# Seven products for six of nine row tiles in layer 0's down-projection of a two-layer encoder step

## The chip, the cores and the metric

The kernel runs on one core of a Trainium2 chip. The metric is device time in microseconds (us) of one execution, the median of several runs. TensorE (PE in the profile) does the matmuls, VectorE (DVE) and ScalarE (ACT) and GpSimd (POOL) the elementwise work, and all transfers between the chip's memory and its on-chip buffer are issued by SyncE (SP).

## The reference

One inference step of a two-layer encoder over 1024 prompt rows and 8 x 16 sample rows, 1152 rows of 1024 columns in all. Layer 0 uses windowed attention, layer 1 a chunk-band attention over a K/V that is projected once after layer 0. Each layer closes with a GEGLU ConvFFN:

```python
u = h @ w_up                     # 1024 -> 2 * 2816
y = conv_b + sum(conv_w[tap] * ue[:, tap:tap + T] for tap in range(3))
a, g = split(y, 2)
f = (gelu(g) * a) @ w_down       # 2816 -> 1024: the down-projection
x = layer_norm(alpha * x + (1 + gate) * f)
```

The change concerns `@ w_down` of layer 0. Everything is float32; the kernel gets float32 accuracy from reduced operands by splitting each into a high part (a cast) and a low part (the difference), and adding three products: low x high, high x low, high x high.

## The kernel before

The 1152 rows are nine tiles of 128; tile 8 holds the sample rows. The inner dimension 2816 is 22 chunks of 128 (`NFF`), or 11 pairs 2m, 2m+1 (`NK`). The stages follow one another: attention, output projection, `ffn` with its up stage and its down stage, for layer 0 and then layer 1. A planner that simulates the engines (`schedule_with_timeline_sim`) sets each engine's order from the program order and the dependences; `issue_after` pins single instructions. Each engine then runs its list in order, and a `Ring` hands out buffers in turn: a load into a slot waits until the last reader of that slot is done.

**Up stage.** Chunks 0 and 1 go through `plain`, chunks 2 to 21 through `spair`: the up-projection of a chunk and its gate in seven products instead of eight (a Strassen-Winograd scheme), whose weight sums `presum` forms on POOL. `conv_row` applies the convolution, `gated` gelu and the gate (one POOL multiply per chunk, L1357) and stores the chunk to `actD`. In layer 0 the up stage also streams adaLN weights (`ada`, L240) as background work through the same ring of raw slots. In layer 1, `act_sums` (L1370 to L1375) forms on POOL the sums of two chunks' activations and stores them to `actS`, and `weight_sums` (L1378 to L1386) the sums of two chunks of `w_down`, stored to `wT`; `wsum` lists the chunks at which they are placed.

**Down stage of layer 1** (`down2`). Rows 0 to 511 against rows 512 to 1023, and chunk 2m against 2m+1 and column half against column half, form a 2 x 2 block product in seven products (numbered 1 to 7) of 11 steps; tile 8 rides along as a plain fifth tile. A step's operands are read from `actD` or `actS` and from `w_down` or `wT`, split by ScalarE (L183) and VectorE (L194), and multiplied on line L1627.

**Down stage of layer 0** (`down`). Three groups of three tiles, `GR`, each over all 22 chunks with both column halves in six banks. `fetch` loads a whole weight chunk (512 kB; high part on ScalarE, low part on POOL) and three tiles of the chunk's activations (192 kB; low part on VectorE, L1495), and `mm` (L1502) does 18 matmuls of 512 columns. The last group keeps its last four chunks (`KEEP`) back and ends tile by tile, so that `tail` of one tile runs beside the next one's matmuls. `tail` adds the residual (L1521) and calls `norm_tail`: layer norm on VectorE, transposes on TensorE (L1043) and the hidden rows for the next stage, which go to `H` and to `hD`.

The next stage (`kv`) reads the tiles in the order in which the groups finish, forms its own sums of the hidden rows (`tsums`), and needs these for its K products (L1237).

Slots of the seven-product form are half a weight chunk (512 columns, high and low), made by `subslots`:

```python
def subslots(self, ws):
    return Ring([tuple(w[i][:, h * 512 : h * 512 + 512] for i in range(2)) for w in ws for h in range(2)])
```

Of the kernel before, what the change touches and what calls it, by code (L numbers as in the profile page):

```python
# [31 lines left out]
LV = ((0, 1, 2, 8, 3, 4, 5, 6, 7), (0, 1, 2, 6, 7, 8, 3, 4, 5))  # L32
GR = ((0, 1, 2), (6, 7, 8), (3, 4, 5))
GB = ((6, 7, 0, 1, 2, 3), (4, 5, 6, 7, 0, 1), (2, 3, 4, 5, 6, 7))
TBG = ((2, 3), (0, 1), (0, 1))
NPL = 2
NK = NFF // 2
TAILS = ({1: 8}, {0: 0, 2: 1, 5: 2, 8: 3}, {})
# [67 lines left out]
class Trunk:  # L106
# [255 lines left out]
    def vproj(self, l, qs, banks, tmp, cut=NT):  # L362
        ws = [[self.wload(self.I[("wv0", "wv1")[l]][q, i]) for i in range(2)] for q in qs]
        for part in (LV[l][:cut], LV[l][cut:]):
# [478 lines left out]
    def kv(self, hmring):  # L843
# [46 lines left out]
        order = (0, 1, 2, 6, 7, 8, 3, 4, 5)  # L890
# [361 lines left out]
    def ffn(self, l, xsrc, xdst, affs):  # L1252
# [18 lines left out]
        ys = Ring([F[:, o : o + 1152] for o in (10492, 6396, 7548)])  # L1271
        yact, ygate = ys.items[0], ys.items[1:3]
# [82 lines left out]
        def gated(j, ya, yg):  # L1355
            nc.scalar.activation(yg, yg, AF.Gelu_apprx_tanh)
            nc.gpsimd.tensor_mul(yg, yg, ya)  # L1357
            if l == 0 or j % 2:
                nc.sync.dma_start(self.actD[j], yg)
                if l:  # L1360
                    self.pend.append(j // 2)
            else:
                for r in (slice(0, 512), slice(1024, 1152)):
                    nc.sync.dma_start(self.actD[j][:, r], yg[:, r])

        def act_sums():
            for m in self.pend:
                a11, a21 = ygate[0][:, 0:512], ygate[0][:, 512:1024]
                a12, a22 = ygate[1][:, 0:512], ygate[1][:, 512:1024]
# [4 lines left out]
                for i in range(2):  # L1374
                    nc.sync.dma_start(self.actS[m, i], ygate[i][:, 0:1024])  # L1375
# [12 lines left out]
        def plain(j):  # L1388
            y = [yact, ygate[j % 2]] if l else [ys.next(), ys.next()]
# [8 lines left out]
        sub = self.subslots(self.wslots[3:4] + self.wslots[l:3])  # L1398
# [6 lines left out]
        def spair(j, loaded=None, src=None, ready={}):  # L1405
# [5 lines left out]
            def after(i, q):  # L1411
# [6 lines left out]
                if l and i == 1:  # L1418
                    act_sums()
                if l and i == 2 and j in wsum:  # L1420
                    with self.tc.issue_after(pairdma):
                        weight_sums(wsum.index(j))
                if q == 4:
                    y.append(ygate[j % 2] if l else ys.next())
# [3 lines left out]
            ya = yact if l else ys.next()  # L1428
            row(ua, j, 0, ya)
            gated(j, ya, y[0])  # L1430

        self.pend = []
        wsum = list(range(4, 9)) + list(range(10, NFF - 1, 2))
        for j in range(NPL):
            plain(j)
        if l:
            self.take_w0(F32)
# [25 lines left out]
        else:  # L1463
            self.down(l, xsrc, xdst, affs)

    def down(self, l, xsrc, xdst, affs):
        nc, I, F = self.nc, self.I, self.F
        z = Ring([F[:, o : o + 1024] for o in (1152, 2176, 3200)])
        self.hf = F[:, 4224:5248]
        self.zt = F[:, 5248:6272]  # L1470
        self.gateS, self.gateP = F[:, 6272:7296], F[:, 7296:8320]
        xr = Ring([F[:, o : o + 1024] for o in ((8320, 9344) if l else (8320,))])
        spare = F[:, 9344:10368]
        self.lng, self.lnb = F[:, 10368:11392], F[:, 11392:12416]
        narrow = self.ws
        slots = narrow.items + [F[:, 0:1024]]
        self.ws = Ring(slots + [self.hf if l else spare], slots + [F[:, 11644:12668], F[:, 8700:9724]])
        acts = Ring([(self.X1[:, i * 768 : i * 768 + 384], self.X1[:, i * 768 + 384 : i * 768 + 768]) for i in range(6)])
        ws = self.wslots
        order = [ws[2], ws[3], ws[0], ws[1]] + [tuple(self.X1[:, o + 1024 * a : o + 1024 * a + 1024] for a in range(2)) for o in (4608, 6656)]  # L1480
        if l == 0:
# [598 lines left out]
```

## Time and profile before

| | |
|---|---|
| median of 3 runs | 2729.5 us (2723.69 to 2732.46) |
| the profiled execution | 2725.63 us |
| its span, first to last instruction | 2723.8 us, 47309 instructions |
| TensorE busy, granted clock | 96%, 0.99 |
| VectorE, ScalarE, POOL busy | 71%, 50%, 39% |
| layer 0's up-stage products (L1237), from | 523.4 us of the span, up to the down stage |
| layer 0's down stage (first to last of L1502) | 1024.1 to 1304.6 us |
| layer 1's up-stage products (L1237), last | 2479.0 us |
| layer 1's down stage (first to last of L1627) | 2460.8 to 2707.9 us |

A row of the engine windows gives a stretch of the span, its length, each engine's busy time with its number of instructions, then the granted TensorE clock, the busy share of the DMA engines and what they moved. A row of the groups gives line, engine, operation, what is written and read, shape, count, then busy time, mean nanoseconds of one, idle time before it and what ended that. A row of the timeline gives start, length, engine, line, operation; in brackets the idle time before it and what ended it. A row of waits reads "engine, tile, line <- who it waited for: total, times, longest".

### The profile page before, as it was taken

The page shows a single profiled execution, that of the slowest core. Times are in us where ns is not written, and L with a number is a line of the kernel's source. Part 1 is how long each engine was busy: PE and PEld are TensorE (multiplying, and loading weights), DVE is VectorE, ACT ScalarE, POOL GpSimd, SP SyncE. Part 2 cuts the span into 40 slices and gives each one's busy share as a digit, 9 for nine tenths or more (in the row PEclk, how much of TensorE's full clock was granted, in tenths as well). Part 3 has the DMA queues.
Part 4 walks back from the last instruction along what each step waited for, and adds up shares of the span by engine and source line. Part 5 has one row for each costly group of instructions (what it writes and reads, how often), then busy time and mean ns, then how long its engine had stood idle before and what let it go on. Part 6 is the DMA issues. An engine that isn't in the chain of part 4 may idle for free. (4 is left out here: it accounts for less than half of the span.)

```text
span 2723.8 us, 47309 instructions
## 1 busy us (share of the span) xinstructions
PE 2626.5 (96%) x17394; PEld 2344.4 (86%) x17394; DVE 1936.0 (71%) x3846; ACT 1348.5 (50%) x2777; POOL 1068.0 (39%) x771
## 2 busy tenths in 40 slices
PE   7999889999999999999999999989989999999997
PEld 6997768989999998887898888867889999998886
DVE  4476767776677675757864677776878877878668
ACT  3475733443333344444446666672445554546553
POOL 3032523444434357675220121252467666552101
PEclk9999899999999999999999999989999999999999
DMA  9656434644444447666658556774445334349673
GB/s 330 205 156 204 143 111 169 229 164 141 143 155 139 153 138 242 221 219 217 248 189 275 147 150 192 204 241 139 162 148 186 139 126 140 122 145 307 215 238 124
DMA packets 229385, 498.29 MB, mean 183 GB/s; under 512 B 37441, under 2 KB 98961, under 8 KB 229153
## 3 DMA queue, kind: packets, MB, share of 16 engines
q1 hardware_dynamic: 229152, 495.27, 55.3%
q8 instruction: 137, 2.24, 0.3%
q14 instruction: 96, 0.78, 0.1%
HBM read 378.15 MB, written 126.47 MB: 185 GB/s over the span
## 5 line engine op out<-in xcount | busy, mean ns | idle before, releaser
L1237 PE MATMUL PS<-H,wh 128*128 128x256 f32 (+1 forms) x2304 | 352.0, 294 | 0.0
L1237 PEld LDWEIGHTS PS<-H,wh 128*128 128x128 f32 x2304 | 319.3, 188 | 0.0
L1197 DVE TENSOR_TENSOR F<-PS,F 128x256 f32<-128x256 f32 (+1 forms) x446 | 197.3, 452 | 156.0 <-PE PS L1237 149.3
L194 DVE TENSOR_TENSOR wl<-F,wh 128x512 fp32r<-128x512 f32 (+2 forms) x205 | 201.4, 994 | 44.8 <-ACT wh L183 44.4
L183 ACT CAST wh<-F 128x512 fp32r<-128x512 f32 (+3 forms) x221 | 135.5, 625 | 196.8 <-PE PS L1237 89.8
L1237 PE MATMUL PS<-H,wl 128*128 128x320 f32 (+1 forms) x1152 | 201.2, 295 | 6.5 <-DVE wl L194 4.0
L1237 PEld LDWEIGHTS PS<-H,wl 128*128 128x128 f32 x1152 | 168.7, 188 | 12.5 <-issue 5.9
L1237 PE MATMUL PS<-xa,wh 128*128 128x320 f32 (+1 forms) x1168 | 179.2, 294 | 0.0
L1237 PEld LDWEIGHTS PS<-xa,wh 128*128 128x128 f32 x1168 | 162.5, 189 | 0.0
L647 POOL TENSOR_TENSOR F<-F,x2r 64x512 f32<-64x512 f32 x62 | 79.2, 1278 | 206.9 <-DVE F L623 179.4
L1495 DVE TENSOR_TENSOR xa<-xa 128x384 fp32r<-128x384 f32 x66 | 97.7, 1492 | 81.9 <-ACT xa L183 80.3
L183 ACT CAST wh<-ws 128x512 fp32r<-128x512 f32 (+1 forms) x123 | 90.8, 744 | 110.9 <-PE PS L1237 49.3
L1357 POOL TENSOR_TENSOR F<-F 128x1152 f32<-128x1152 f32 x44 | 124.7, 2833 | 43.9 <-DVE F L1350 21.3
L313 PE MATMUL PS<-H,w0r 128*128 128x384 f32 (+1 forms) x720 | 136.9, 340 | 0.0
L1286 DVE SCALAR_TENSOR_TENSOR F<-F 128x1024 f32<-128x1024 f32 (+2 forms) x160 | 132.3, 878 | 5.8 <-ACT F L1325 5.0
L326 PE MATMUL PS<-xa,H 128*128 128x512 f32 x504 | 129.3, 397 | 5.2 <-ACT xa L183 3.3
L525 DVE CUSTOM_DVE_ANT_0 F<-PS,F,C 128x256 f32<-128x256 f32 (+3 forms) x208 | 97.3, 480 | 50.3 <-PE PS L561 26.9
L313 PE MATMUL PS<-H,wh 128*128 128x384 f32 (+1 forms) x672 | 132.8, 339 | 0.0
L313 PEld LDWEIGHTS PS<-H,w0r 128*128 128x128 f32 x720 | 124.5, 188 | 1.6 <-DVE F L633 0.4
L587 PE MATMUL PS<-C,F 128*128 128x128 f32 x720 | 112.7, 280 | 6.9 <-DVE C L636 3.1
L326 PE MATMUL PS<-wh,H 128*128 128x512 f32 (+1 forms) x468 | 117.4, 359 | 0.7 <-ACT wh L183 0.5
L529 ACT ACTIVATE F<-F,C 128x640 f32<-128x640 f32 (+5 forms) x144 | 95.3, 663 | 44.9 <-DVE C L525 42.9
(361 smaller groups left out, 6944.6 us busy)
## 6 DMA issues: line engine op xcount, KB each, us to landing
ws<-in_adaw_dram SPq DMA_DIRECT2D x63, 512.0 KB
ws<-in_wup_dram SPq DMA_DIRECT2D x51, 512.0 KB
F<-in_adaw_dram SPq DMA_DIRECT2D x49, 512.0 KB
actD<-F SPq DMA_DIRECT2D x33, 576.0 KB
F<-in_wup_dram SPq DMA_DIRECT2D x37, 512.0 KB
ws<-in_wdn_dram SPq DMA_DIRECT2D x33, 512.0 KB
F<-in_wdn_dram SPq DMA_DIRECT2D x33, 512.0 KB
xa<-kH SPq DMA_DIRECT2D x60, 256.0 KB
```

The costliest lines, as they stand in the source:

```text
L183: nc.scalar.copy(out, in_)
L194: self.eng(el).tensor_sub(lo, src, hi.bitcast(F32))
L313: mm = self.nc.tensor.matmul(out[:, 0:n], w[a][:, k * 128 : k * 128 + 128], H[:, p, k, s0 : s0 + n], start=i == 0, stop=i == 23)
L326: self.nc.tensor.matmul(out[:, 0:n], H[:, p, j * kn + k, t0 : t0 + 128], w[a][:, k * n : k * n + n], start=i == 0, stop=i == 23,)
L525: nc.vector.tensor_tensor_reduce(out=p[:, c0 : c0 + w], in0=ps, in1=b, scale=1.0, scalar=init, op0=ALU.add, op1=ALU.min, accum_out=nm)
L529: self.lastexp = nc.scalar.activation(p[:, 0:n], p[:, 0:n], AF.Exp, bias=nm, scale=-1.0, accum_out=rs).ins
L587: nc.tensor.transpose(t[:, n * 128 : n * 128 + 128], p[:, (kt - k0) * 128 : (kt - k0) * 128 + 128], self.ident)
L1197: nc.vector.tensor_add(d, v(ps), a if len(a.shape) == 3 else v(a))
L1237: self.pairmm = nc.tensor.matmul(ps[:, 0:m], w[a][:, k * 128 : k * 128 + 128], x(p, k, n), start=start and c == 0, stop=c == 11, skip_grou ...
L1286: nc.vector.scalar_tensor_tensor(o, u, cw[:, cc, i : i + 1], o, op0=ALU.mult, op1=ALU.add)
L1357: nc.gpsimd.tensor_mul(yg, yg, ya)
L1495: nc.vector.tensor_sub(lo, raw, hi.bitcast(F32))
```

## The change

Layer 0 forms the same kind of sums as layer 1 in its up stage, in a variant for three tiles against three (`HALF` is 384 columns there): tiles 0 to 2 against tiles 3 to 5. `weight_sums` has four subtractions for layer 0 and stores all four halves to `wT`; it runs on chunks 5, 7, 9, 10, 11, 13, 14, 15, 17, 18, 19. The `w0` buffer holds the raw sums and is no longer a weight slot of layer 0's up stage. The row buffers are `yact` and two `ygate` in both layers. The last chunk's gate multiply goes from POOL to VectorE.

The new `down1` replaces `down`. Products 1, 2, 5, 6, 3, 7, 4 run over 11 steps with three tiles and one column half each (9 matmuls a step). The last two steps of each are kept back and end tile by tile (four in product 4), and `done` reads each bank as it ends. Tiles 0 to 2 are complete after product 3 and are normed in product 7; tiles 3 to 5 after product 4 and are normed in the plain group. The group of tiles 8, 6, 7 (`GR`) goes last, plainly, over 22 chunks with 18 matmuls each; its first two chunks are loaded ahead of product 4's kept matmuls. Before product 4 the rings of slots are made anew. The next stage's tile order follows.

```diff
-LV = ((0, 1, 2, 8, 3, 4, 5, 6, 7), (0, 1, 2, 6, 7, 8, 3, 4, 5))
-GR = ((0, 1, 2), (6, 7, 8), (3, 4, 5))
+LV = (0, 1, 2, 8, 3, 4, 5, 6, 7)
+GR = (8, 6, 7)
+GB = (2, 3, 4, 5, 6, 7)
+TBG = (0, 1)
+HALF = (384, 512)
+WSUM = ((5, 7, 9, 10, 11, 13, 14, 15, 17, 18, 19), (4, 5, 6, 7, 8, 10, 12, 14, 16, 18, 20))
...
-        order = (0, 1, 2, 6, 7, 8, 3, 4, 5)
+        order = (0, 1, 2, 3, 4, 5, 8, 6, 7)
...
-            nc.gpsimd.tensor_mul(yg, yg, ya)
-            if l == 0 or j % 2:
+            (nc.vector if l == 0 and j == NFF - 1 else nc.gpsimd).tensor_mul(yg, yg, ya)
+            if j % 2:
                 nc.sync.dma_start(self.actD[j], yg)
...
+            if l == 0:
+                nc.gpsimd.tensor_sub(b11, b12, b11)
+                nc.gpsimd.tensor_sub(b12, b22, b12)
+                nc.gpsimd.tensor_sub(b22, b22, b11)
+                nc.gpsimd.tensor_sub(b21, b22, b21)
+                for i in range(2):
+                    nc.sync.dma_start(self.wT[m, i], self.w0[i])
+                return
...
-        sub = self.subslots(self.wslots[3:4] + self.wslots[l:3])
+        sub = self.subslots(self.wslots[3:4] + self.wslots[1:3])
...
-        if l:
-            self.take_w0(F32)
+        self.take_w0(F32)
...
+        raws = [w[:, i * 512 : i * 512 + 512] for w in narrow.items for i in range(2)]
+        raws += [F[:, 0:512], F[:, 512:1024], self.w0[1][:, 512:1024]]
+        early, late = Ring(raws + [F[:, 1024:1536]]), Ring(raws)
+        subs = Ring(self.subslots(ws[1:4]).items + [(X1[:, o : o + 512], X1[:, o + 512 : o + 1024]) for o in range(3072, 9216, 1024)])
+        lows = [(H[:, 0, c, 384:768], H[:, 1, c, 384:768]) for c in range(8)]
+        highs = [(H[:, 0, c, 768:1152], H[:, 1, c, 768:1152]) for c in range(8)]
+        acts = Ring([(X1[:, o : o + 384], X1[:, o + 384 : o + 768]) for o in range(0, 3072, 768)] + lows + highs)
...
+        def weight(src, ring=None):
+            hi, lo = subs.next()
+            raw = ring.next() if ring else lo.bitcast(F32)
+            nc.sync.dma_start(raw, src)
+            self.split(raw, hi, lo, "a", "v")
+            return hi, lo
+
+        def act(src):
             hi, lo = acts.next()
             raw = lo.bitcast(F32)
+            nc.sync.dma_start(raw, src)
+            self.split(raw, hi, lo, "a", "v")
+            return hi, lo
...
+        def product(q, banks, new=True, keep=0, hook=None, ahead=lambda: None, done=lambda i: None):
+            for m in range(NK - keep):
+                a, w = fetch(q, m)
+                for i in range(3):
+                    mm(self.bank(banks[i]), a, i, w, new and m == 0, m == NK - 1)
+                if hook:
+                    hook(m)
+            kept = [(m, *fetch(q, m)) for m in range(NK - keep, NK)]
+            ahead()
+            for i in range(3):
+                for m, a, w in kept:
+                    mm(self.bank(banks[i]), a, i, w, new and m == 0, m == NK - 1)
+                done(i)
...
+        A, B, C = (0, 1, 2), (5, 6, 7), (2, 3, 4)
...
+        product(1, A, hook=start, keep=2, done=to_p1)
+        aff = affs()
+        product(2, A, new=False, keep=2, done=to_c11)
+        product(5, B, keep=2, done=to_q5)
+        product(6, B, new=False, keep=2, done=to_u4)
+        for t in range(3):
+            fetch_row(t)
+        product(3, B, new=False, keep=2, done=to_c12)
...
+        product(7, C, keep=2, hook=done, done=to_c22)
+        subs, acts = Ring(subs.items[4:12]), Ring(lows)
...
+        def ahead():
+            nonlocal acts
+            self.ws, acts = Ring(plain), Ring(highs)
+            firsts.extend(load(j) for j in range(2))
...
+        product(4, B, keep=keep, hook=more, ahead=ahead, done=to_c21)
+        rows = []
+        for j in range(NFF - keep):
+            w, a = firsts[j] if j < 2 else load(j)
+            for i, t in enumerate(GR):
+                block(j, w, a, i, t)
+            if j == 0:
+                for i in range(3):
+                    gate(q5[i], q5[i], 3 + i, 0)
+                    gate(u4[i], u4[i], 3 + i, 1)
+                    rows.append(head(3 + i))
+                self.take_w0(F32R)
+                self.wring.items.append(ws[0])
+            if j in (1, 5, 9):
+                norm(4 + j // 4 - 1, rows[j // 4], hf1)
```

Here `done(m)` of product 7 norms tiles 0, 1, 2 at steps 0, 3, 7; `to_p1` and `to_q5` are copies by ScalarE, `to_c11`, `to_u4`, `to_c12`, `to_c22`, `to_c21` one or two VectorE instructions of 128 x 512 a tile.

More of the change, by code (lines that the diff above doesn't have):

```diff
@@ L363, in vproj @@
         ws = [[self.wload(self.I[("wv0", "wv1")[l]][q, i]) for i in range(2)] for q in qs]
-        for part in (LV[l][:cut], LV[l][cut:]):
+        for part in (LV[:cut], LV[cut:]):
             for q, w in zip(qs, ws):
@@ L1565, in down @@
         self.ws = narrow
-        if not l:
-            self.wring = Ring(ws)
+        self.wring = Ring(ws)
+        self.X2 = self.x2p.tile([128, 4608], F32R, name="x2r", tag="x2")
     def down2(self, l, xsrc, xdst, affs, act_sums):
```

229 lines of the change are left out of this document (124 added, 105 removed).

## The prediction

> **What bounds the kernel now.** I read the page's busy shares, then the engines by stretches of time, then the down-projection's own rows, and last what TensorE waits for there.
>
> ```profile
> span 2723.8 us, 47309 instructions
> PE 2626.5 (96%) x17394; PEld 2344.4 (86%) x17394; DVE 1936.0 (71%) x3846; ACT 1348.5 (50%) x2777; POOL 1068.0 (39%) x771
> ...
> core 0: us, PE busy (x) PEld busy (x) DVE busy (x) ACT busy (x) POOL busy (x), PEclk, DMA share, GB/s
> 600.00:1000.00 400.00, 398.13 (x3170) 367.88 (x3170) 278.56 (x417) 153.09 (x258) 163.70 (x123) 1.00 0.43 146
> 1024.00:1304.60 280.60, 278.60 (x1241) 227.82 (x1240) 185.11 (x212) 117.92 (x174) 179.66 (x70) 1.00 0.66 220
> 2070.00:2460.00 390.00, 389.45 (x2949) 388.86 (x2948) 305.92 (x512) 198.61 (x392) 239.77 (x181) 1.00 0.41 142
> 2480.00:2500.00 20.00, 20.00 (x88) 16.42 (x89) 18.33 (x17) 11.27 (x21) 13.67 (x9) 1.00 1.00 341
> 2500.00:2645.00 145.00, 145.00 (x636) 119.12 (x635) 95.61 (x145) 79.80 (x132) 12.63 (x9) 1.00 0.73 242
> ```
>
> The five stretches are layer 0's up stage, its down stage, layer 1's up stage, and the start and body of layer 1's down stage. TensorE is full in each at a granted clock of 1.00, so a matmul taken out is worth its issue interval, as long as no operand is late. Layer 1 already runs what layer 0 is to get: sums formed in the up stage, seven products in the down stage. Its rows price most of the change.
>
> ```profile
> 1024.00:1304.70 280.70, 273.51 (x1188) 222.40 (x1188) 1.00 0.66 220
> ...
> 1106.20 8.18 PEld L1502 LDWEIGHTS PS<-xa 128*128 128x128 f32 x36
> ...
> 1114.41 0.64 PEld L1502 LDWEIGHTS PS<-x2r,xa 128*128 128x128 f32 x3
> ...
> PE PS L1043 <- ACT F L1059: 2.0, 6, 0.6
> ```
>
> The first row is the down-projection's own line, 1188 matmuls; 36 weight loads start 8.21 us apart in sum, 0.228 us each, and 1188 x 0.228 = 270.9 of the stage's 280.6 us. The only TensorE wait of note is 2.0 us at transposes.
>
> **The change, part by part. Matmuls.** Tiles 0 to 5 cost 22 x 6 x 2 x 3 = 792 matmuls of 512 columns; seven products of 11 steps with 3 tiles and 3 passes cost 693. Tiles 8, 6, 7 keep 396. So 99 go: 99 x 0.228 = 22.6 us, all on the path. This is the whole gain.
>
> **Loads and splits in the products.** One step now has 9 matmuls, 2.05 us, and needs 384 columns of activations and 512 of weights split.
>
> ```profile
> L1495 DVE TENSOR_TENSOR xa<-xa 128x384 fp32r<-128x384 f32 x60 | 88.9, 1489 | 80.1 <-ACT xa L183 78.6 <-PE PS L1502 1.5
> ...
> 1286.67 0.55 DVE L1495 TENSOR_TENSOR xa<-xa 128x384 fp32r<-128x384 f32 x1
> ...
> L183 ACT CAST xa<-xa 128x384 fp32r<-128x384 f32 x60 | 30.9, 514 | 68.7 <-DMA xa<-actD 67.7 <-DVE F L1515 1.0
> ...
> L194 DVE TENSOR_TENSOR H<-H 128x512 fp32r<-128x512 f32 x22 | 15.0, 690 | 11.4 <-ACT H L183 11.4
> ...
> L183 ACT CAST H<-H 128x512 fp32r<-128x512 f32 x22 | 13.4, 619 | 13.7 <-DMA H<-actS 8.5 <-DMA H<-wT 5.0
> ...
> L1515 DVE TENSOR_TENSOR F<-PS,F 128x512 f32<-128x512 f32 x18 | 11.9, 684 | 8.3 <-PE PS L1502 8.3
> ```
>
> VectorE takes 0.55 + 0.69 = 1.24 us a step while POOL is idle, ScalarE 0.51 + 0.62 = 1.13: both under 2.05. The product stretch lasts 693 x 0.228 = 158 us; splits fill 77 x 1.24 = 95 us of VectorE there, the 21 evictions, gates and sums of 128x512 at 0.684 another 14. DMA needs 196.6 + 262.1 = 459 kB per 2.05 us, 224 GB/s, where 341 has been seen. SP issues two loads a step; over the stage 77 x 2 + 22 x 2 = 198 where it issued 132, 0.38 us each by the rows below: 75 of 268 us. These are hidden in the mean. At the start of the stage they are not sure to be: layer 1's first 20 us have VectorE at 18.33 and DMA at 1.00 with a step of 12 to 15 matmuls, and here a step is 9.
>
> ```profile
> 2479.96 1.20 PE L1627 MATMUL PS<-wh,xa 128*128 128x512 f32 x4 [0.71 <-ACT wh L183]
> ```
>
> That start cost layer 1 0.7 us. The last pair's activation sums (POOL) and its final product with gelu, now on VectorE, fall there too. Bounds 0 and 4 us; I take 2, nearer layer 1's row. The five seams where a bank is read between two products have 6 matmuls, 1.37 us, of other tiles as cover (the last two steps end tile by tile) against 0.684: 1 us in all, bounds 0 and 2.
>
> **Norms of tiles 0 to 2 in product 7.** One norm's long instructions on VectorE:
>
> ```profile
> 1307.70 1.22 DVE L1521 SCALAR_TENSOR_TENSOR F<-F 128x1024 f32<-128x1024 f32 x1
> ...
> 1301.72 1.28 DVE L994 BATCH_NORM_STATS2 C<-F 128x6 f32<-128x512 f32 x2
> ...
> 1317.60 0.81 DVE L1033 TENSOR_SCALAR F<-F,C 128x1024 f32<-128x1024 f32 x1
> ...
> 1320.84 1.37 DVE L1051 TENSOR_SCALAR F<-PS,C 128x128 f32<-128x128 f32 x4 [2.43 <-PE PS L1043]
> 1322.12 1.22 DVE L1066 TENSOR_TENSOR F<-F 128x1024 f32<-128x1024 f32 x1
> 1323.37 1.23 DVE L1067 TENSOR_TENSOR F<-F 128x1024 f32<-128x1024 f32 x1
> ```
>
> 7.1 us, with the single-column ones about 8 (an estimate), three times 24. (The low part of the hidden rows is split on POOL, as before.) Product 7 lasts 11 x 2.05 = 22.6 us. Its own splits can be done ahead (12 weight and 20 activation slots), so TensorE need not feel it; but VectorE leaves product 7 about as late as TensorE does. Over the whole stretch VectorE has 95 + 14 + 24 = 133 of 158 us.
>
> **The seam from product 7 to product 4.** Here the rings are cut: `subs` restarts at its item 4, `acts` at the first low slot. Each fetch takes one item, so product 7's fetches are numbers 55 to 65; modulo 12 its two kept steps (64, 65) hold items 4 and 5, modulo 20 they hold low slots 0 and 1. These are exactly what product 4's first two steps load into. Those loads wait on SP until product 7's last matmuls, and a load landing, a cast and a subtraction follow before TensorE can go on. Two loads of this size that the split really waited for:
>
> ```profile
> 2558.28 0.38 SPq L1611 DMA_DIRECT2D wl<-wT  x1
> ...
> 2561.38 0.62 ACT L183 CAST wh<-wl 128x512 fp32r<-128x512 f32 x1 [0.70 <-DMA wl<-wT]
> ...
> 2562.04 0.69 DVE L194 TENSOR_TENSOR wl<-wl,wh 128x512 fp32r<-128x512 f32 x1 [0.15 <-ACT wh L183]
> ...
> 2562.82 0.38 SPq L1611 DMA_DIRECT2D wl<-wT  x1
> ...
> 2567.48 0.62 ACT L183 CAST wh<-wl 128x512 fp32r<-128x512 f32 x1 [1.65 <-DMA wl<-wT]
> ...
> 2568.13 0.69 DVE L194 TENSOR_TENSOR wl<-wl,wh 128x512 fp32r<-128x512 f32 x1 [1.47 <-ACT wh L183]
> ```
>
> From issue to the end of the split: 4.45 and 6.0 us. Step 9's slots come free 0.7 us before the product ends, so TensorE stands 3.8 to 5.3 us, more if the split queues behind a norm. I take 5. Nothing else is ready for TensorE: the plain group's matmuls come after. Behind the waiting loads on SP stand steps 2 on and residual rows; behind the waiting cast on ScalarE and the subtraction on VectorE the same steps' splits; for all of these TensorE has 2.05 us of work a step, so they cost nothing more.
>
> **The seam from product 4 to the plain group.** The plain group's first two steps (four loads, two casts of 1024 and of 384 columns, the subtractions, now on VectorE for the weights) are issued ahead of product 4's kept 36 matmuls, 8.2 us, into slots that product 7 has left; its banks 2 to 4 are read in product 4, banks 5 to 7 tile by tile with 12 matmuls, 2.7 us, between them. I cost it at nothing; if product 7's norms push VectorE back, this seam is late next.
>
> **Layer 0's up stage.** Added on POOL: 11 x 4 weight sums of 512 columns and 11 x 4 activation sums of 384; on SP, 22 weight loads, 22 + 22 stores and 11 more activation stores, fewer bytes in those; two weight slots (six halves instead of eight) and one row buffer go.
>
> ```profile
> L1383 POOL TENSOR_TENSOR w0f<-w0f 128x512 f32<-128x512 f32 x9 | 14.1, 1567 | 0.5
> ...
> L1373 POOL TENSOR_TENSOR F<-F 128x512 f32<-128x512 f32 x9 | 13.9, 1544 | 0.1
> ...
> L1357 POOL TENSOR_TENSOR F<-F 128x1152 f32<-128x1152 f32 x16 | 43.3, 2707 | 8.1 <-DVE F L1286 7.9
> ...
> L1357 POOL TENSOR_TENSOR F<-F 128x1152 f32<-128x1152 f32 x18 | 52.4, 2914 | 28.7 <-DVE F L1350 19.4 <-issue 3.9 <-ACT F L1204 1.8
> ```
>
> 44 x 1.57 + 44 x 1.54 x 384/512 = 120 us, 6 a pair. The last two rows are one per pair: 16 in 600 to 1000, 25 us a pair; 18 in 2070 to 2460, 21.7. POOL goes from 163.7/16 = 10.2 to 16.2 of 25 us, 65%; layer 1 has 239.77/18 = 13.3 of 21.7, 61%, the same smaller buffers, and TensorE 389.45 of 390. That is the cover. Unlike layer 1, layer 0 also streams adaLN weights through SP, and its matmuls stand in TensorE's own order:
>
> ```profile
>   DMA ws<-in_adaw_dram: 10.5, 11
> ```
>
> Over the whole kernel these waits are 10.5 us, mostly at the opening. If a store waiting on POOL delays such a load, TensorE waits. Bounds 0 (layer 1) and 10 us; I take 2, nearest layer 1.
>
> **The end of the stage.** Tile 8 moves into the last group, where its norm has 16 instructions in place of four:
>
> ```profile
> L1078 DVE TENSOR_TENSOR F<-F,C 128x128 f32<-128x128 f32 x8 | 6.2, 833 | 0.0
> ...
> L1077 DVE TENSOR_TENSOR F<-PS,C 128x128 f32<-128x128 f32 x8 | 1.7, 278 | 0.0
> ...
> 1369.93 4.38 PE L1237 MATMUL PS<-xa,w0r 128*128 128x320 f32 x20 [1.88 <-DVE xa L194]
> ```
>
> 8.9 against 1.4 us on VectorE, shortly before the next stage's T sums, for which TensorE already waits. It is first of its group, with the other two's kept matmuls behind it, 48 x 0.228 = 11 us. Bounds -1 (the sums' order also changes) and 4; I take 1. Everything else (order lists, constants, the last product's engine) is nothing or counted.
>
> **Sum.** -22.6 + 2 + 1 + 5 + 2 + 1 = -11.6 us. The profiled execution took 2725.6 us, its span 2723.8 and 1.8 around it: it would become 2714.0. It is 3.9 under the median 2729.5, which becomes 2718.
>
> **Rivals.** *Bubble hidden* (the loads land early or the order puts work there): -22.6 + 6 = -16.6, 2713, down to 2707 if the other terms vanish too. For: TensorE idles little anywhere. Against: the slot numbers.
>
> *VectorE bound.* Products 7 and 4 last 45 us; norms 24, evictions and sums 15 x 0.684 = 10, product 4's splits and the plain group's first two activations 11 x 1.24 + 2 x 0.55 = 15, its first two weights (four halves of 0.69) 2.8: 52. If nothing is done ahead, product 7's own 11 splits add 14. That is over by 7 to 21 us, a change of -5 to +9; I take 2730, no change. Against: ring depth, and the norms may slip into the plain group.
>
> *Up stage late* (ends slower). Place: layer 0's splits behind POOL.
>
> ```profile
> L194 DVE TENSOR_TENSOR wl<-F,wh 128x512 fp32r<-128x512 f32 x59 | 61.3, 1049 | 24.2 <-ACT wh L183 24.1
> ```
>
> The same split takes 1.05 us here and 0.69 where POOL is idle. Each of 20 pairs losing 1.5 us gives +30 - 11.6 = +18, 2748; from 1 us a pair it decides against the change. Against: VectorE needs 278.56/16 = 17.4 of 25 us, so even 6 us more leave room. [...]
>
> **Chances.** Forecast 0.50 (its own range 2711 to 2721), bubble hidden 0.15, VectorE bound 0.20, up stage late 0.15. 0.3% is 8.2 us, about what a measurement tells from no change. Faster: 0.15 + 0.48 = 0.63; same: 0.02 + 0.17 + 0.04 = 0.23; slower: 0.03 + 0.11 = 0.14. Range 2707 to 2736: above it lie the late up stage's worse cases, below it nothing likely.
>
> **What would show it.** The down stage's own line with 1089 matmuls in about 268 us from first to last; one TensorE wait of 4 to 7 us on a split some 150 us into the stage, with SP's load issued at product 7's end; POOL near 65% in layer 0's up stage with TensorE still full, and that stage as long as now. Wrong if TensorE idles in each pair, or if VectorE is at 100% through products 7 and 4.

## The result and the profile after

The change made the kernel slower: 2754.2 us (median of 6 runs, 2744.0 to 2759.4) against 2728.1 beside it, a ratio of 1.0092, 95% interval 1.0070 to 1.0114. The forecast was 2718, range 2707 to 2736. The profiled execution took 2744.0 us, the fastest of the six, so its trace accounts for 18.4 us of the 26 (span 2742.2 against 2723.8).

The top of the page, then the engines by stretches (the first row is layer 0's up stage before the change, the second the same stage after it, the others are all of after), then what TensorE waited for in the new down stage (total, times, longest):

```profile
span 2742.2 us, 47674 instructions
...
PE 2617.6 (95%) x17295; PEld 2334.3 (85%) x17295; DVE 2001.8 (73%) x3980; ACT 1361.5 (50%) x2849; POOL 1081.8 (39%) x812
```

```profile
core 0: us, PE busy (x) PEld busy (x) DVE busy (x) ACT busy (x) POOL busy (x), PEclk, DMA share, GB/s
523.62:1024.24 500.62, 490.09 (x3890) 455.10 (x3889) 354.19 (x530) 196.55 (x333) 212.31 (x154) 1.00 0.46 156
...
521.04:1049.44 528.40, 502.05 (x3889) 462.13 (x3889) 386.36 (x539) 194.63 (x336) 326.02 (x230) 0.98 0.59 203
...
600.00:1000.00 400.00, 386.35 (x3029) 353.33 (x3028) 288.94 (x390) 142.66 (x244) 272.85 (x192) 0.99 0.59 205
1049.40:1324.00 274.60, 260.79 (x1140) 211.93 (x1139) 213.96 (x329) 137.50 (x250) 81.07 (x32) 0.98 0.72 244
...
1189.00:1209.00 20.00, 16.95 (x79) 13.09 (x79) 20.00 (x31) 9.29 (x18) 6.60 (x2) 1.00 0.89 313
1209.00:1229.00 20.00, 17.93 (x78) 14.11 (x77) 15.91 (x18) 9.15 (x15) 11.05 (x5) 1.00 0.60 220
1229.00:1249.00 20.00, 18.71 (x88) 15.07 (x86) 19.96 (x33) 8.98 (x18) 14.98 (x6) 1.00 0.50 171
1249.00:1269.00 20.00, 14.50 (x57) 11.89 (x58) 15.76 (x17) 8.62 (x15) 11.71 (x5) 0.83 0.65 228
```

```profile
PE PS L1045 <- ACT F L1061: 6.8, 1, 6.8
PE PS L1516 <- ACT x2s L1586: 1.9, 1, 1.9
PE PS L1516 <- DVE xa L196: 1.8, 1, 1.8
PE PS L1516 <- DVE w0f L1602: 1.6, 2, 1.3
PE PS L1516 <- ACT F L1061: 1.5, 1, 1.5
```

Layer 0's up stage, full before, now has 386 busy us of TensorE in 400. Two stages are compared below by their lengths in the trace: "up" from layer 0's first pair product to the first matmul of its down-projection, "down" from there to that projection's last matmul. Up went from 500.6 to 528.4 us (+27.8), down from 280.0 to 274.2 (-5.8). What lies ahead of and between the stages and in layer 1 makes the rest: -2.6, -1.9, +1.5 and -0.6 us. So the removed 99 matmuls should have given 22.6 us in the down stage, of which 17 were lost there; the loss came from the stage that forms the sums.

Not all of it is waiting. In the up stage TensorE's idle time grew from 10.5 to 26.4 us, and its busy time, for the same work, from 490.1 to 502.1, at a granted clock of 0.98 instead of 1.00. So about 16 of the 27.8 us are waits, and 12 are the same matmuls taking longer. In the down stage idle time grew from 2.0 to 13.8 us, and some 5 us more went the second way.

**How a pair of the up stage gets late.** The pair with products from 758.73 us, the longest behind the stage's first two (29.9 us instead of 24.0), in the timeline of the changed kernel (start, length, engine, line; in brackets the idle time before and what ended it). L1166 to L1169 are the operand sums of `presum`, L1373 and L1374 sums of activations, L1384 to L1387 weight sums:

```profile
754.21 1.29 POOL L1168 TENSOR_TENSOR F<-ws 128x512 f32<-128x512 f32 x1
...
755.46 1.02 POOL L1373 TENSOR_TENSOR F<-F 128x384 f32<-128x384 f32 x1
...
755.53 0.62 ACT L185 CAST wh<-F 128x512 fp32r<-128x512 f32 x1 [6.79 <-POOL F L1168]
...
756.43 1.74 POOL L1384 TENSOR_TENSOR w0f<-w0f 128x512 f32<-128x512 f32 x1
...
758.13 1.27 POOL L1167 TENSOR_TENSOR F<-F,ws 128x512 f32<-128x512 f32 x1
...
758.73 0.86 PE L1239 MATMUL PS<-H,wl 128*128 128x320 f32 x4
...
759.36 1.02 POOL L1374 TENSOR_TENSOR F<-F 128x384 f32<-128x384 f32 x1
...
759.44 1.14 ACT L185 CAST wh<-F 128x512 fp32r<-128x512 f32 x2 [3.29 <-POOL F L1167]
760.09 2.54 DVE L196 TENSOR_TENSOR wl<-F,wh 128x512 fp32r<-128x512 f32 x2 [2.34 <-ACT wh L185]
760.34 1.75 POOL L1385 TENSOR_TENSOR w0f<-w0f 128x512 f32<-128x512 f32 x1
...
762.05 1.73 POOL L1169 TENSOR_TENSOR ws<-ws,F 128x512 f32<-128x512 f32 x1
...
762.96 3.18 DVE L1288 SCALAR_TENSOR_TENSOR F<-F 128x1024 f32<-128x1024 f32 x2
...
766.06 0.41 DVE L1199 TENSOR_TENSOR F<-PS,F 128x256 f32<-128x256 f32 x1
...
766.57 1.35 ACT L1327 ACTIVATE F<-F 128x1152 f32<-128x1152 f32 x1 [4.12 <-DVE F L1199]
...
767.92 0.69 ACT L1206 COPY F<-PS 128x320 f32<-128x320 f32 x2
...
768.38 0.90 PE L1239 MATMUL PS<-H,wl 128*128 128x320 f32 x2 [3.14 <-ACT F L1206]
```

Between the second and the fourth operand sum POOL now runs two activation sums and two weight sums. The third operand sum (L1167) ends at 759.4, 0.7 us after its pair has begun; before the change it ended 4.5 us ahead. ScalarE's cast waits 3.3 us for it with everything behind it, VectorE's splits wait for the casts, and the evictions L1199 and the taps behind the splits are late; ScalarE's next row waits 4.1 us for the second of these evictions, the PSUM copy L1206 stands behind it, and TensorE, whose bank it frees, stands 3.1 us. After that wait its granted clock is 0.50 for 5.7 us, and the 192 matmuls of this pair take 26.7 busy us instead of 24.0:

```profile
768.38:774.10 5.72, 5.72 (x24) 5.72 (x24) 5.44 (x9) 2.33 (x4) 1.74 (x3) 0.50 0.65 240
```

The fourth sum ends at 763.8, 5.1 us into the pair, and nothing here waits for it; below, its end serves as the mark of how far POOL's list is behind. What this pair shows goes for the whole stage. ScalarE's waits for the third sum (from 560 us on) and TensorE's for the PSUM copy (in the whole stage), each before and after the change:

```profile
ACT wh L183 <- POOL F L1165: 8.8, 14, 1.1
...
ACT wh L185 <- POOL F L1167: 31.7, 18, 3.3
...
PE PS L1237 <- ACT F L1204: 1.0, 1, 1.0
...
PE PS L1239 <- ACT F L1206: 14.9, 11, 3.1
```

The last two rows hold 13.9 of the 15.8 us by which TensorE's idle time grew.

**Why layer 1's cover did not hold.** Rows of the kernel before, POOL's last operand sum (L1167) and the first matmul of its pair, in layer 0 and then in layer 1 (there the matmuls of neighbouring pairs mix; the row is the later of the two that can be the first):

```profile
745.09 1.29 POOL L1164 TENSOR_TENSOR F<-ws 128x512 f32<-128x512 f32 x1 [8.21 <-DMA ws<-in_wup_dram]
...
749.41 1.62 POOL L1167 TENSOR_TENSOR ws<-ws,F 128x512 f32<-128x512 f32 x1
...
753.79 0.86 PE L1237 MATMUL PS<-H,wl 128*128 128x320 f32 x4
...
2200.18 1.30 POOL L1167 TENSOR_TENSOR F<-F 128x512 f32<-128x512 f32 x1
...
2217.86 0.75 PE L1237 MATMUL PS<-H,wl 128*128 128x320 f32 x4
```

In layer 0 the sums start when their weights land and end 2.8 us before the pair; in layer 1 they end 16 us before it. From the third pair on, save the last, this lead was 2.2 to 9.4 us in layer 0 in the trace of before (about 4.4 in most); in layer 1, where a pair's start is known only to a few us, it was some 10 to 20. Layer 1's POOL was the busier, 61% against 41%, but its lead of 10 us and more is what its own sums on POOL leave; the 4 us of layer 0 stood without any, and 6 us of added work a pair do not fit into them.

### The profile page after: what moved, and what is told of

Its sections match the earlier page's. It is cut to its first block, busy times and chain, and to the rows that moved or that the text cites. A ratio compares the mean times of both kernels' runs of the same rounds, so it can differ in the third digit from the quotient of the medians.

```text
span 2742.2 us, 47674 instructions
## 1 busy us (share of the span) xinstructions
PE 2617.6 (95%) x17295; PEld 2334.3 (85%) x17295; DVE 2001.8 (73%) x3980; ACT 1361.5 (50%) x2849; POOL 1081.8 (39%) x812
## 5 line engine op out<-in xcount | busy, mean ns | idle before, releaser
L1239 PE MATMUL PS<-H,wh 128*128 128x320 f32 (+1 forms) x2624 | 403.5, 295 | 0.0
L1239 PEld LDWEIGHTS PS<-H,wh 128*128 128x128 f32 x2624 | 366.4, 189 | 0.0
L196 DVE TENSOR_TENSOR wl<-F,wh 128x512 fp32r<-128x512 f32 (+2 forms) x236 | 232.6, 995 | 77.1 <-ACT wh L185 73.8
L1199 DVE TENSOR_TENSOR F<-PS,F 128x256 f32<-128x256 f32 (+1 forms) x446 | 196.1, 452 | 121.6 <-PE PS L1239 114.7
L185 ACT CAST wh<-F 128x512 fp32r<-128x512 f32 (+2 forms) x239 | 140.8, 601 | 261.9 <-PE PS L1239 121.9
L1239 PE MATMUL PS<-H,wl 128*128 128x320 f32 (+1 forms) x1312 | 232.8, 299 | 22.4 <-ACT F L1206 17.2
L1239 PE MATMUL PS<-xa,wh 128*128 128x320 f32 (+1 forms) x1328 | 204.0, 295 | 0.0
L196 DVE TENSOR_TENSOR H<-H 128x384 fp32r<-128x384 f32 (+2 forms) x144 | 115.5, 815 | 60.2 <-ACT H L185 59.8
L196 DVE TENSOR_TENSOR wl<-ws,wh 128x512 fp32r<-128x512 f32 (+1 forms) x118 | 120.3, 1021 | 25.8 <-ACT wh L185 21.8
L185 ACT CAST H<-H 128x384 fp32r<-128x384 f32 (+3 forms) x158 | 94.9, 610 | 85.2 <-DMA H<-actD 40.8
L1239 PE MATMUL PS<-xa,wl 128*128 128x256 f32 (+1 forms) x664 | 120.7, 303 | 7.4 <-DVE F L1199 5.2
```

The costliest lines, as they stand in the source:

```text
L185: nc.scalar.copy(out, in_)
L196: self.eng(el).tensor_sub(lo, src, hi.bitcast(F32))
L1199: nc.vector.tensor_add(d, v(ps), a if len(a.shape) == 3 else v(a))
L1239: self.pairmm = nc.tensor.matmul(ps[:, 0:m], w[a][:, k * 128 : k * 128 + 128], x(p, k, n), start=start and c == 0, stop=c == 11, skip_grou ...
```

## The experiments

The first theory was POOL: the added sums take its time, or stand in its order ahead of what TensorE needs, or hold VectorE. The rival was what comes with the sums: transfers, stores that the single row buffers wait for, fewer weight slots. In the down stage the bubble stood against VectorE held by POOL. Ratios are to the kernel before, run on the same chip, with 95% intervals; stage lengths are those of each kernel's profiled execution.

| kernel | ratio | up us | down us |
|---|---|---|---|
| before | 1 | 500.6 | 280.0 |
| changed | 1.0092 (1.0070 to 1.0114) | 528.4 | 274.2 |
| both sums 8 columns | 0.9992 (0.9974 to 1.0009) | 502.2 | 270.2 |
| weight sums 8 columns | 0.9987 (0.9975 to 0.9999) | 503.2 | 272.6 |
| activation sums 8 columns | 1.0017 (1.0002 to 1.0031) | 511.0 | 271.3 |
| taps through PSUM | 1.0059 (1.0034 to 1.0084) | 514.1 | 281.7 |
| sums in another order | 1.0068 (1.0053 to 1.0083) | 518.5 | 273.8 |
| weight sums on VectorE | 1.0085 (1.0067 to 1.0103) | 527.1 | 275.6 |
| rings rotated | 1.0051 (1.0035 to 1.0067) | 528.1 | 264.6 |
| plain low parts on VectorE | 1.0052 (1.0037 to 1.0067) | 528.2 | 260.9 |
| order, rings, low parts | 1.0018 (1.0006 to 1.0030) | 523.3 | 257.1 |
| VectorE late, rings, low parts | 1.0012 (0.9997 to 1.0028) | 521.6 | 258.0 |
| order, rings, low parts, PSUM | 0.9980 (0.9966 to 0.9995) | 505.5 | 262.3 |
| the first of these, spread | 0.9989 (0.9973 to 1.0005) | 518.1 | 256.6 |
| spread, PSUM save last pair | 0.9960 (0.9949 to 0.9972) | 509.6 | 259.3 |

In the two kernels with all taps through PSUM the planner drew 30 matmuls of the down-projection into the last pair, whose products end 9 and 12 us after "up" does; there up and down have to be taken together. The six kernels that have the changed kernel's down stage unedited, those two left out, took 270.2 to 275.6 us in it; differences of that size say nothing.

### Which sums

```diff
             if l == 0:
+                b11, b12, b21, b22 = (b[:, 0:8] for b in (b11, b12, b21, b22))
                 nc.gpsimd.tensor_sub(b11, b12, b11)
...
+                if l == 0:
+                    a11, a12, a21, a22 = (a[:, 0:8] for a in (a11, a12, a21, a22))
                 nc.gpsimd.tensor_add(a22, a21, a22)
```

Both edits:

> The changed kernel with the added sums of layer 0's up stage cut to 8 of 512 and 8 of 384 columns (most of the sums are left out); every load, store, wait and buffer stays. If POOL's time for the sums (124 us in that stage) makes the stage longer, the stage from its first pair product to the down stage's first matmul falls from 528 us to about 502 (500.6 before the change) and the kernel takes about 2725 us. If the single row buffers and the stores' waits, the added DMA or the fewer weight slots do it, the stage stays at 520 or more and the kernel at 2745 or more.

The first alone:

> The changed kernel with only the weight sums of layer 0 cut to 8 columns (83 of the added 124 us of POOL; these sums are left out). If the loss goes with POOL's time, two thirds of it come back: the up stage at about 510 us, the kernel at 2735. If it is the activation sums, which hold the row buffers that the next pair's taps write, the stage stays near 525 and the kernel near 2750.

The second alone:

> The changed kernel with only the activation sums of layer 0 cut to 8 columns (41 of the added 124 us of POOL; these sums are left out). If the loss goes with POOL's time, a third comes back: the up stage at about 519 us, the kernel at 2745. If the row buffers held by these sums are the cause, the stage falls to about 505 and the kernel to 2730.

The stage came back to 502.2 with both, 503.2 with the weight sums alone cut and 511.0 with the activation sums alone. The stretch of the up stage without the weight sums' work:

```profile
600.00:1000.00 400.00, 398.54 (x3176) 368.55 (x3175) 282.15 (x417) 153.96 (x259) 226.89 (x204) 1.00 0.61 212
```

TensorE is full again although every load, store and buffer stayed and DMA's share is 0.61. So transfers, row buffers and fewer weight slots cost about 2 us together, and POOL's work the rest. It does not go with POOL's time in proportion: a third of the work taken away gave back 17 us, two thirds gave 25, all of it 26. The activation sums alone fit beside the operand sums (503.2 against 502.2 without either); the weight sums alone cost 9 us, and both together 26.

### Where the sums stand on POOL

```diff
+        self.pre = E.tensor_sub(a21, a12, S2).ins
...
+            if part == 0:
+                with self.tc.issue_after(self.pre):
+                    nc.gpsimd.tensor_sub(b11, b12, b11)
+                    nc.gpsimd.tensor_sub(b12, b22, b12)
+                return
+            with self.tc.issue_after(self.gmul):
+                nc.gpsimd.tensor_sub(b22, b22, b11)
+                nc.gpsimd.tensor_sub(b21, b22, b21)
```

> The changed kernel with the same sums on the same engine in another order on POOL: the first two of a pair's four weight sums stand right behind the four operand sums of the next pair, the other two behind the next gated product. Nothing is left out; POOL has the same work. If the loss comes from weight sums that stand ahead of operand sums which TensorE's next products need (order), most of it goes: up stage 503 to 510 us instead of 528, the kernel about 2728 to 2735. If the sheer time of POOL or its hold on VectorE does it, the stage stays at 520 or more and the kernel near 2750.

Ten of the 27.8 us came back, with the same work; neither theory's number. Pair by pair it is clearer: from the third to the fifteenth pair all but one (26.0) took 23.9 to 25.6 us, and two later pairs (30.6 and 31.6 us) carried most of what was left. Ahead of the first of them POOL waited 3.0 us for the store of the rows that its activation sums work on, these then stood between the operand sums, and the fourth of those ended 2.9 us into the pair.

### The weight sums on VectorE

```diff
-                nc.gpsimd.tensor_sub(b11, b12, b11)
+                nc.vector.tensor_sub(b11, b12, b11)
...
```

> The changed kernel with the 44 weight sums of layer 0 on VectorE instead of POOL; nothing is left out. Two-operand instructions of this size took VectorE 0.69 us when POOL was idle, so 30 to 48 us more on VectorE (73% busy) and 83 less on POOL. If POOL's time or order is the cause, the up stage is 502 to 508 us and the kernel 2725 to 2730. If VectorE's own queue is the limit in a pair, four sums in a row ahead of evictions or splits cost 1 us a pair again: stage 515 or more, kernel 2740.

Nothing was gained, with 83 us less for POOL. The waits of VectorE in that kernel say what happened:

```profile
DVE w0f L1384 <- DMA w0f<-in_wdn_dram: 36.7, 11, 5.4
```

Each first weight sum stood 3.3 us for its rows to land, with splits, taps and evictions behind it. That these waits ate the gain is argued and not shown: the run that was to take them away (below) kept them.

### Taps through PSUM

```diff
-        cb, sb = Ring([6, 7]), Ring([1, 3, 5])
+        cb, sb = Ring([6, 7] if l else [6]), Ring([1, 3, 5])
...
-            row = conv_row_psum if l else conv_row
+            row = conv_row_psum
```

> The changed kernel with layer 0's row convolution done as in layer 1: the partial rows stand in PSUM bank 6, so that VectorE's taps of 512 columns read one operand from PSUM; all sums stay, nothing is left out. If VectorE's taps held by POOL (two operands in SBUF on both engines) carry the loss, the up stage falls to 500 to 508 us and the kernel to about 2728 to 2735. If POOL's queue itself is late for the operand sums, whatever VectorE does, the stage stays at 520 or more and the kernel at 2745 or more. A single PSUM bank for both rows could also cost ScalarE or VectorE waits of its own, 1 to 2 us a pair.

Some of the loss came back, between the two numbers for the kernel (2741.6 us). "Up" reads 14 us less, but 30 matmuls of the down-projection stand in its last pair, whose products end 526.0 us after the stage's start (528.3 in the changed kernel). Without these 30, 6.8 us at 0.228, it is 519.2, a gain of 9; up and down together gained 6.8. The taps by shape (busy time, mean ns of one), first in the changed kernel between 560 and 1000 us, then in this one:

```profile
L1288 DVE SCALAR_TENSOR_TENSOR F<-F 128x1024 f32<-128x1024 f32 x66 | 94.7, 1435 | 7.4 <-ACT F L1327 7.0
L1288 DVE SCALAR_TENSOR_TENSOR F<-F 128x120 f32<-128x120 f32 x33 | 23.1, 699 | 0.0
```

```profile
L1288 DVE SCALAR_TENSOR_TENSOR PS<-F,PS 128x512 f32<-128x512 f32 x70 | 52.7, 753 | 21.9 <-ACT PS L1350 21.8
L1344 DVE SCALAR_TENSOR_TENSOR F<-F,PS 128x120 f32<-128x120 f32 x34 | 11.3, 331 | 0.5
```

The taps of 120 columns fall from 0.70 to 0.33 us. Those of 1024 took 1.28 us in the changed kernel where POOL ran for less than a tenth of them and 1.57 where it ran for more than half; those of 512 that read PSUM 0.75 in either case (so did layer 1's in the changed kernel: 0.75 with POOL at less than a tenth of them, 0.75 at more than half). So POOL's hold on the taps is gone. This cannot be parted from POOL's lateness: its instructions up to the stage's last pair product took 290 us instead of 326, and from the third pair on two fourth sums ended after their pair's start instead of nine. What is left of the loss from there on is not explained by late sums, and its cause stays open; ScalarE stood 60.5 us for the single bank, as the expectation feared.

### The down stage's two suspects

Product 4's slots in another order:

```diff
-        subs, acts = Ring(subs.items[4:12]), Ring(lows)
+        subs, acts = Ring(subs.items[6:12] + subs.items[4:6]), Ring(lows[2:8] + lows[0:2])
```

> The changed kernel with product 4's slots in another order (weights from item 6, activations from the third low slot), so that its first loads need not wait for product 7's last matmuls; nothing is left out. If the prediction's bubble is there, TensorE's waits between 1187 and 1202 us (about 5.6 us, with the matmuls of the plain group drawn into it) go and the down stage is 268 to 270 us instead of 274.3. If VectorE, with three norms in product 7, is what is late there, nothing changes (273 to 276).

The plain group's low parts:

```diff
-            w = self.wload(wdn[j], el="v" if j < 2 else EL)
+            w = self.wload(wdn[j], el="v")
```

> The changed kernel with the low parts of all plain-group weights split on VectorE instead of POOL; nothing is left out. If POOL's 1024-column subtractions hold VectorE's (2.7 us for a 384-column split that takes 0.55 alone), the TensorE gap of 8 us near 1247 goes and the down stage is 266 to 269 us instead of 274.3. If VectorE is simply full with norms, evictions and splits, 22 x 1.3 us more on it make the plain group later: stage 274 to 280 us.

The first took 9.6 us off the stage, the second 13.3, both more than expected. Not all of the 9.6 is the edit's: TensorE's wait of 1.9 us at 1072, between products 1 and 2, and the low clock behind it are gone too, and the edit does not touch them. With the rings rotated the waits at 1190 and 1202 us went, but TensorE still stood twice for product 4's evictions (L1606) on VectorE, 6.8 us. The changed kernel's timeline around the long gap shows why VectorE is late there; L196 on POOL is a 1024-column low part of a plain weight, L1035 and L1053 belong to the norms, L1061 copies a bank of transposes out, and TensorE's next transposes wait for it:

```profile
1237.58 0.80 DVE L1035 TENSOR_SCALAR F<-F,C 128x1024 f32<-128x1024 f32 x1
...
1238.85 2.40 POOL L196 TENSOR_TENSOR w0r<-F,w0r 128x1024 fp32r<-128x1024 f32 x1 [5.02 <-ACT w0r L185]
...
1239.10 2.71 DVE L1035 TENSOR_SCALAR F<-F,C 128x1024 f32<-128x1024 f32 x1
...
1244.02 2.89 POOL L196 TENSOR_TENSOR xa<-F,xa 128x1024 fp32r<-128x1024 f32 x1
...
1244.54 8.01 DVE L196 TENSOR_TENSOR H<-H 128x384 fp32r<-128x384 f32 x3
...
1252.47 1.35 DVE L1053 TENSOR_SCALAR F<-PS,C 128x128 f32<-128x128 f32 x4
...
1253.86 0.58 ACT L1061 COPY F<-PS 128x512 f32<-128x512 f32 x1 [7.28 <-DVE F L1053]
...
1254.50 1.12 PE L1045 MATMUL PS<-C,F 128*128 128x128 f32 x4 [6.79 <-ACT F L1061]
```

A normalising instruction that takes 0.80 us alone takes 2.7 beside POOL, a split of 384 columns 2.67 instead of the 0.55 seen with POOL idle: here they last about as long as POOL's instructions beside them, 2.40 to 2.89 us. Some 12 of VectorE's 19.96 busy us in 1229 to 1249 are instructions held in this way; with the low parts on its own list, 1.22 us each in the rows of that trace from 1225 to 1230, it had more to do and was hardly late: TensorE's idle time in the stage fell from 13.8 to 4.0 us.

### Together

Order on POOL (with `WSUM` 4, 6, 8, 10, 11, 12, 14, 16, 17, 18, 20), rings and low parts:

> The changed kernel with three edits, nothing left out: the weight sums behind the operand sums and the gated product as in the ordered run, and now mostly in pairs without activation sums; product 4's slots rotated; all low parts of plain-group weights on VectorE. If a pair is slow only where its operand sums end after its start, the up stage is 500 to 508 us (518.5 with the order alone, where two such pairs stayed); if the two down-stage effects add, that stage is 256 to 259 us. Kernel about 2708 to 2716, below both kernels. If POOL's time counts whatever its order, the up stage stays at 515 or more and the kernel at about 2722.

The same with the sums on VectorE, one behind each of the next pair's first four products:

> As the run before it, but the weight sums on VectorE, one behind each of the next pair's first four products, when their rows have long landed; nothing left out. In the earlier run on VectorE it stood 36.7 us in 11 waits for those rows' DMA. If these waits were what cost there, the up stage falls from 527 to 501 to 506 us, with the down stage at 256 to 259, the kernel at 2706 to 2714. If VectorE has no room for 3 us more in a pair, the up stage stays above 515.

The first with the taps through PSUM:

> The first of these three with layer 0's row convolution through PSUM bank 6 besides; nothing left out. If VectorE's taps held by POOL still cost something in the right order, the up stage is 2 to 6 us shorter than in the first. If the single bank's waits cost more than the hold (ScalarE waited 60 us for it in the earlier run), it is 3 to 10 us longer.

The down stage took 257.1 us, as expected, 23 less than before the change; the two single effects would add up to 251.3, so they overlap. In the up stage both first runs missed, at 523.3 and 521.6, where their rivals had put them (515 or more). (In the second, where pairs with weight sums adjoin, four last sums read rows of the next load, so its output is not the reference's; the work is the same. These sums again stood 31.6 us for their rows, so it does not tell whether VectorE has room.) In the first, the third to tenth pairs took 23.9 to 25.4 us; the long ones (26.7, 26.8, 28.9, 29.9, 28.0) stood where weight sums were in adjoining pairs, 10 to 12 and 16 to 18, or at the end. Through PSUM up and down together took 767.8 us against 780.4: the 2 to 6 us expected of it were too few.

### Spread, and the best version

`WSUM` of 3, 4, 5, 6, 8, 10, 12, 14, 16, 18, 20:

> The run with the order mended and the down stage mended, with the weight sums spread otherwise: in pairs 3 to 6 and then every second pair to 20, none in neighbouring pairs after the 6th; nothing left out. In the traces so far pairs whose operand sums ended 2 us or more before them took 24.8 us, those with sums more than 2 us late 28.6. If that lateness alone sets the loss, the pairs after the 6th are 25 us with sums 2 us early, the up stage is 502 to 510 us, the down stage 257, the kernel 2708 to 2715. If the sum of POOL's work makes the sums late however it is spread, the stage stays at 515 to 523 us and the kernel at 2724 to 2730.

The same through PSUM:

```diff
+            row = conv_row if l == 0 and j == NFF - 1 else conv_row_psum
```

> The same with layer 0's row convolution through PSUM, save in the last pair, which took 32.7 us with it and 22 to 28 without; nothing left out. If both lateness and the hold on VectorE count, the up stage is 496 to 503 us, the down stage 257 to 262, the kernel 2702 to 2712, faster than the kernel before the change by 0.5 to 0.9%. If the spread already does everything, it equals the first run within 3 us.

Spread, eleven of the twelve pairs from the seventh to the eighteenth took 23.9 to 25.0 us, the other 26.7, so the spread did what was expected of it there. The stage as a whole took 518.1, the rival's number and not the expected one, though from the seventh pair to the eighteenth the sums were late in three pairs only: the first two pairs (61.4 us against 56.6 before) and the last two (29.1 and 27.9 against 24.9 and 23.1) hold most of the rest. The first two have the plain chunks' activation sums ahead of the second pair's operand sums, which ended 14.3 us late (7.8 before); in the last, VectorE's splits took 1.6 to 1.7 us beside the weight sums of chunk 20, and TensorE waited 3.4 us for the eviction behind them. Moving these was not tried. The down stage, 256.6 us, had one TensorE wait of 1.0 and one of 0.3 us.

With PSUM as well the stage was 509.6, not 496 to 503, and the kernel took 2715.8 us, not 2702 to 2712, yet it is the fastest measured: against 2728.8, a ratio of 0.9960 (0.9949 to 0.9972), 13 us below the kernel before and 1.3% below the changed one.

**All pairs without PSUM taps.** In the twelve traces whose row convolution does not go through PSUM, the fifth to nineteenth pair of each, by the end of their last operand sum (POOL's fourth line of `presum`) against their first matmul:

| operand sums end | pairs | mean length us |
|---|---|---|
| 2 us or more before the pair | 74 | 24.8 |
| 0 to 2 us before | 53 | 25.5 |
| 0 to 2 us into the pair | 33 | 26.1 |
| 2 us or more into it | 20 | 28.1 |

That alone would be a correlation, and this last sum is hardly waited for itself (1.6 us in one wait in the changed kernel); it marks how late POOL's list is. That taking work off this list gave back 17 to 26 us and moving it 10 makes the lateness a cause. It is not all of it: the next to last pair took 28.5 to 29.6 us in six kernels with its sums in time, at a TensorE wait of 4.1 to 4.8 us for an eviction (L1199) behind VectorE's taps. What starts that stays open.

## Why the prediction was wrong, step by step

**Matmuls, -22.6.** Right: 1089 in the stage, and where the stalls are mended it is 23 us shorter.

**Layer 0's up stage, +2 (0 to 10).** This step failed, by 26 us: +27.8. POOL's share was forecast well (65%; it is 272.85 of 400, 68%), and the conclusion from it, that layer 1 with 61% and a full TensorE is cover, was wrong. A busy share says nothing of the due time of one instruction in it. The rows that did were not read: POOL's operand sums in layer 0 waited 8.2 us for their weights and ended 2.8 us before their pair began. What the +2 stood for, an adaLN load that comes late, was there and small: TensorE's wait for one grew from 2.0 to 3.6 us.

**The price of a wait.** A TensorE wait was priced at its length, with the clock at 1.00 throughout. In the up stage 15.8 us of added idle time came with 12.0 us of slower matmuls, a term that the sum does not have.

**The rival "up stage late", 0.15.** It was what happened, in place and about in size: 27.8/20 = 1.4 us a pair where 1.5 was supposed. Its argument against, 6 us of room on VectorE, was void for the same reason. Of its two parts, POOL's lateness and its hold on VectorE, both showed: another order gave 10 us, taps through PSUM 7 to 9, neither all.

**Start of the down stage, +2, and seams, +1.** No wait at the start. The seam from product 1 to product 2 alone cost 1.9 us in this trace, behind ScalarE's copy of the bank, and 1.6 more at a lower clock (below).

**The bubble from product 7 to 4, +5.** In part. Product 4's load was issued at 1191.3, at product 7's end, as the step said. But the one wait of 4 to 7 us on a split did not come: TensorE waited 1.3, 0.3 and 1.5 us at 1190, 1194 and 1202, for product 7's evictions (L1602) and for a copy of transposes (L1061). The step said that nothing else was ready for TensorE; in fact the planner had drawn matmuls of the plain group into the gap, and the transposes of the norms stood there too.

**The plain group and norms, 0.** Failed: 1.8 us at the seam and 6.8 at the transposes, from POOL's low parts. The same rows stood in the prediction (1.49 us mean for a 384-column split, 0.55 alone), priced in product 7, where POOL is idle, and not in the plain group.

**Norms of tiles 0 to 2 hidden in product 7.** Right: with rings and low parts mended they stayed where they were and the whole stage had 1.3 us of TensorE waits. "VectorE bound" named the right engine, at 100% in 1189 to 1209, but not the cause of the long gap: there VectorE was held by POOL, and more work on VectorE instead of POOL made the stage shorter.

**End of the stage, +1.** From the last matmul of the down-projection to layer 1's first pair product the trace has 708.3 us before and 706.4 after; within what the traces differ by (706 to 710), so nothing to see.

## What to carry to other kernels

Before work is added to an engine that looks idle, find in the trace the instructions on its list that others wait for, and measure how long before their use they end: that lead, not the idle share, is the room. Added work goes behind those instructions by an explicit order, spread over steps, and with its rows landed before its turn comes: here the first weight sums on VectorE stood 36.7 us for theirs in 11 waits. Where long instructions of POOL run beside VectorE, price VectorE's by what the trace shows beside them and not alone: here a split of 384 columns took 2.67 us beside POOL's 2.65 to 2.89, and 0.55 alone. Price a TensorE wait at its length, and with the clock as an upper bound: behind a wait of 1.9 us the slower clock cost 1.6 us more here, behind one of 3.1 us 2.7.

## What was not expected of the hardware

**The clock fell after some short waits.** The engines by stretches in the changed kernel, around the 1.9 us for which TensorE stood at 1072:

```profile
1072.00:1076.00 4.00, 2.10 (x6) 1.39 (x6) 4.00 (x8) 1.74 (x4) 0.00 (x0) 0.81 1.06 387
1076.00:1080.00 4.00, 4.00 (x15) 3.14 (x15) 1.86 (x4) 1.81 (x4) 0.90 (x1) 0.77 0.98 374
...
1254.00:1258.00 4.00, 3.50 (x11) 2.92 (x12) 3.96 (x3) 1.39 (x2) 2.53 (x1) 0.50 0.82 233
```

The eight matmuls after that wait were issued every 0.43 us instead of 0.23, 1.6 us more; after the 6.8 us wait eight more, at a granted clock of 0.50. A wait of 1.8 us at 1220 had no such price: the clock is 1.00 in the stretch 1209 to 1229 above. Nor had one of 2.9 us at 559 in the kernel before, with 1.00 on both sides of it. So of two waits of 1.8 and 1.9 us one cost 1.8 and the other 3.5 us; 1.9 us were enough for a fall in one case and 2.9 not in another.

**A one-input instruction was held too.** L1035 reads one tensor of the on-chip buffer and still went from 0.80 to 2.7 us beside POOL, in two cases. Not every one was: two of L996, which reads one tensor as well, beside POOL's instruction at 1228.15 took 0.67 and 0.68 us, as against 0.69 in the mean with POOL idle. The hold works the other way too here: POOL's 1024-column subtraction at 1204.8, beside a run of two-operand instructions on VectorE, took 6.86 us instead of 2.4.
